# A diffusion block on one core: the input projection's first chunk in one written order with eight banks, its weights on GpSimd's queue, and another order of the first norm and dots

## The chip, the cores and the metric

The kernel runs on one core of a Trainium2 chip, in one launch. The metric is the device time of one execution in microseconds. The engines are TensorE (PE: matmuls; its weight loads are listed as PEld), VectorE (DVE), ScalarE (ACT), GpSimd (POOL) and SyncE (SP), which here only issues DMAs; GpSimd and ScalarE can issue them too.

## What is computed

One block of a latent transformer in f32 with 512 latent tokens, 256 context tokens and a width of 2048. What matters here is its start:

```python
mod_l = silu(c) @ w_ada + b_ada          # 6 * 2048 values: shift, scale, gate, twice
mod_c = silu(c_ctx) @ w_ada + b_ada
h_l = rms_norm(x, g_mix_norm) * (1 + sc_a) + sh_a       # 512 x 2048
p = h_l @ w_in                                          # 512 x 3904
```

Behind it come the context's part of the projection, attention, short convolutions, the output projection with a residual, and a gated MLP with a second norm; the change does not touch how they are written.

## The kernel before

**Matmuls.** Tokens are the free dimension (512), features lie on the 128 partitions, so x is 16 tiles of 128x512 (`xr0` to `xr15`). Each f32 operand is split into a high and a low part, and a product is three matmuls (`mm3`): high by high (L187), high by low of h (L188), low by high (L189). A weight tile that has landed is cut into pieces of up to 512 columns; ScalarE casts a piece to its high part (L166) and VectorE subtracts it from the raw tile for the low part (L167). The pieces have 4 buffers, and one more that every fifth uses.

**The first norm.** x lands in 16 loads on SP's queue; ScalarE squares each (L351, L354), VectorE adds them up (L355), TensorE sums over the partitions (L316), ScalarE takes the root (L289), VectorE the reciprocal (L291), TensorE spreads it over the partitions (L299), and ScalarE copies the result to `rl`.

**The shifts and scales.** Rows 16+j and j of `w_ada` (scale and shift of tile j) are not multiplied on TensorE: each comes as two halves of 128x1024 (`ada`, 4 buffers), and VectorE takes the dot with silu(c), which lies on all partitions as `sv`, in one instruction for each half (L241); `total` (L235) adds the halves and the bias. `prep(j)` does that for both rows and then makes h of tile j: VectorE multiplies by `rl` (L435), ScalarE applies scale and shift (L438) and casts to the high part (L337), VectorE makes the low part (L338). silu of c (and of c_ctx, as `svc`) is made by four matmuls that spread the row (L413) and four activations (L414).

**The input projection** has 31 blocks of 128 columns and 16 k-tiles. The k-tiles are taken in three chunks of 2, 4 and 10 (`KCH`). In each chunk the first G = 6 blocks go k-tile by k-tile into six banks (`pf`, from `first_banks`), as their h comes; the other 25 go block by block (`pp`). `evac` copies (chunk 0, ScalarE, L539) or adds (chunks 1 and 2, VectorE, L541) a full bank to `acc`. `prep` calls stand between the blocks of chunks 0 and 1; between those of chunk 2 stand the same dots with silu(c_ctx), for the context (L530).

**What sets the order.** A scheduler orders each engine's instructions; an instruction marked with `keep` stays in the written order among the others so marked on its engine. All loads of the first two chunks are kept on SP's queue, in the order of the calls:

```python
raw = load(w_in[:, off:off + k * P], k * P, f"rw{ci}_{m}")   # SP: fetch_to
...
for f, j in todo.get((ci, i), []):
    f(j)                          # prep: four ada loads on SP, then the dots
```

Of the kernel before, what the change touches and what calls it, by code (L numbers as in the profile page):

```python
# [10 lines left out]
F32 = mybir.dt.float32  # L11
# [20 lines left out]
G = 6  # L32

# [39 lines left out]
def block_kernel(ctx, tc, xt, ctxt, ctxn, c, c_ctx, w_ada, small, w_in, w_inc, w_q, w_kv, w_out,  # L73
# [38 lines left out]
    def big(nm):  # L112
        return pp.tile([P, 1024], F32, tag="b", bufs=2, name=nm)
# [15 lines left out]
    def first_banks(nm):  # L129
        turn[:] = 5, None  # L130
        r = [sml(f"{nm}{g}") for g in range(4)]
        b = big(f"{nm}4")
        return r + [b[:, :512], b[:, 512:]]
# [9 lines left out]
    def fetch_to(dst, src):  # L143

        ins = SP.dma_start(dst, src)
        if ordered[0]:
            keep(ins)

    def load(src, n, name):
        nth["raw"] += 1  # L150
        if "raw" in spare and nth["raw"] % 3 == 0:
            raw = spare["raw"].tile([P, 2048], F32, tag="raw", bufs=1, name=name)
        else:
            raw = wp.tile([P, 2048], F32, tag="raw", bufs=2, name=name)
        fetch_to(raw[:, :n], src)
        return raw
# [76 lines left out]
    def total(col, t, dst):  # L233

        V.scalar_tensor_tensor(out=dst, in0=col[:, 0:1], scalar=col[:, 1:2], in1=s("b_ada", t), op0=ALU.add, op1=ALU.add)  # L235

    def dot_v(raw, vec, t, dst, nm):

        col = tiny(2, f"dv{nm}{t}")
        for i, r in enumerate(raw):  # L240
            V.scalar_tensor_tensor(out=r, in0=r, scalar=1.0, in1=vec[:, i * 1024:(i + 1) * 1024], op0=ALU.mult, op1=ALU.mult, accum_out=col[:, i:i + 1])  # L241
        total(col, t, dst)
# [157 lines left out]
    with ExitStack() as pa:  # L400
# [4 lines left out]
        def silu_rows(src, dst, nm):  # L405

            row = wp.tile([P, 2048], F32, tag="raw", bufs=2, name=nm)[0:1, :]
            fetch_to(row, src)
            for g in range(4):
                if g % 2 == 0:  # L410
                    both = big(f"{nm}{g}")
                ps = both[:, (g % 2) * 512:(g % 2 + 1) * 512]
                PE.matmul(ps, ones[0:1, :], row[:, g * 512:(g + 1) * 512], start=True, stop=True)  # L413
                A.activation(dst[:, g * 512:(g + 1) * 512], ps, AF.Silu)  # L414
# [7 lines left out]
        hl = {}  # L422

# [28 lines left out]
        rms([ssq], D, T, rl)
        A.copy(out=ones_r, in_=ones)

        V.tensor_scalar(s("g_q", 0, 4), s("g_q", 0, 4), scalar1=-SCALE, scalar2=None, op0=ALU.mult)
# [101 lines left out]
        todo = {(0, 1 + 6 * i): [(prep, 2 + i)] for i in range(4)}  # L557
# [5 lines left out]
        off = 0  # L563
        for ci, (k0, n) in enumerate(zip(K0, KCH)):

            pss = first_banks(f"pf{ci}")
            if ci == 2:
                bg.append(ctx_stats())
            for q in range(n):
                if ci == 0:  # L570
                    prep(q)
                elif ci == 2:
# [436 lines left out]
    SP.dma_start(sv_d, sv)  # L1009
# [577 lines left out]
def _layout(x, c, ctx, c_ctx, w_ada, b_ada, g_mix_norm, w_in, g_q_a, w_q_b, g_kv_a, w_kv_b,  # L1587
# [25 lines left out]
    for t in range(8):  # L1613
# [57 lines left out]
```

## Time and profile before

| | |
|---|---|
| median of 3 runs | 2134.2 us (2133.86 to 2139.27) |
| the profiled execution | 2139.37 us, its span 2137.6 us |
| granted clock, mean of the span | 0.993 |
| TensorE busy | 2091.0 us of the span |
| VectorE busy | 1826.5 us |
| ScalarE busy | 1047.5 us |
| GpSimd busy | 117.2 us |

The span is the part of the profiled execution that the trace covers. The trace gives for each instruction its start, its duration, and what ended the idle time of its engine before it. "DMA share" is the mean busy share of the core's 16 DMA engines; PEclk is the clock that TensorE was granted, 1.00 being 2.4 GHz and 0.50 being 1.2 GHz.

### The profile page before, as it was taken

The page shows a single profiled execution, that of the slowest core. Times are in us where ns is not written, and L with a number is a line of the kernel's source. Part 1 is how long each engine was busy: PE and PEld are TensorE (multiplying, and loading weights), DVE is VectorE, ACT ScalarE, POOL GpSimd, SP SyncE. Part 2 cuts the span into 40 slices and gives each one's busy share as a digit, 9 for nine tenths or more (in the row PEclk, how much of TensorE's full clock was granted, in tenths as well). Part 3 has the DMA queues.
Part 4 walks back from the last instruction along what each step waited for, and adds up shares of the span by engine and source line. Part 5 has one row for each costly group of instructions (what it writes and reads, how often), then busy time and mean ns, then how long its engine had stood idle before and what let it go on. Part 6 is the DMA issues. An engine that isn't in the chain of part 4 may idle for free.

```text
span 2137.6 us, 35318 instructions
## 1 busy us (share of the span) xinstructions
PE 2091.0 (98%) x13268; PEld 1881.8 (88%) x13268; DVE 1826.5 (85%) x3024; ACT 1047.5 (49%) x1715; POOL 117.2 (5%) x144
## 2 busy tenths in 40 slices
PE   7999999999999999999999999999999999999997
PEld 4688788888988888999999999999999889999997
DVE  7998987778896989898999999999999658888887
ACT  5533333555552337565555555555655433333445
POOL 0000000000000100011000000000000000000000
PEclk9999999999999999999999999999999999999999
DMA  8989886334459986577788888788888989878684
GB/s 331 343 279 329 276 275 195 126 128 152 166 188 353 348 283 220 142 217 207 230 238 232 233 233 244 224 234 234 235 229 229 362 306 307 250 231 239 197 236 134
DMA packets 170177, 513.75 MB, mean 240 GB/s; under 512 B 18963, under 2 KB 23315, under 8 KB 164371
## 3 DMA queue, kind: packets, MB, share of 16 engines
q1 hardware_dynamic: 133364, 418.14, 57.7%
q0 software_dynamic: 17408, 59.25, 14.1%
q10 hardware_dynamic: 19232, 34.09, 4.2%
q8 instruction: 104, 1.70, 0.3%
q14 instruction: 69, 0.56, 0.1%
HBM read 464.22 MB, written 46.14 MB: 239 GB/s over the span
## 4 chain that ended last, share of the span: by engine, by line
PE 90%; DVE 4%; DMA 3%; ACT 2%; issue 1%; SPq 0%; DVEq 0%; ACTq 0%; POOLq 0%
PE pp L187 4%; PE pp L189 4%; PE pp L188 4%; PE d L187 1%; PE o L187 1%; PE d L188 1%; PE o L188 1%; PE d L189 1%; PE o L189 1%; PE uf L187 1%; PE uf L189 1%; PE uf L188 1%; PE of L187 1%; PE of L188 1%; PE of L189 1%; PE pf L188 1%
## 5 line engine op out<-in xcount | busy, mean ns | idle before, releaser
L1151 POOL DMA_DIRECT2D u_s<-in_w_up x80 | 68.6, 857 | 684.0 <-DMA u_s<-in_w_up 378.1
L263 DVE SCALAR_TENSOR_TENSOR ada<-ada,sv 128x1024 f32<-128x1024 f32 x68 | 82.1, 1220 | 11.4 <-DMA ada<-in_w_ada 11.2
L166 ACT CAST w_0h<-rw 128x512 fp32r<-128x512 f32 (+1 forms) x63 | 38.3, 618 | 108.3 <-PE pp L188 67.6
L241 DVE SCALAR_TENSOR_TENSOR ada<-ada,sv 128x1024 f32<-128x1024 f32 x64 | 77.6, 1220 | 2.2 <-DMA ada<-in_w_ada 2.1
L530 DVE SCALAR_TENSOR_TENSOR ada<-ada,svc 128x1024 f32<-128x1024 f32 x64 | 76.0, 1219 | 2.5 <-DMA ada<-in_w_ada 2.4
L167 DVE TENSOR_TENSOR w_0l<-rw,w_0h 128x512 fp32r<-128x512 f32 (+1 forms) x63 | 42.7, 683 | 22.8 <-ACT w_0h L166 22.6
L263 DVE SCALAR_TENSOR_TENSOR ra<-ra,sv 128x1024 f32<-128x1024 f32 x44 | 52.5, 1219 | 1.1 <-DMA ra<-in_w_ada 1.1
L1265 DVE TENSOR_TENSOR u<-u,u_s 128x1024 f32<-128x1024 f32 x40 | 48.8, 1220 | 0.7 <-DMA u_s<-in_w_up 0.5
L1266 DVE TENSOR_TENSOR u<-u,u 128x1024 f32<-128x1024 f32 x40 | 48.7, 1218 | 0.0
L793 POOL TENSOR_TENSOR gr<-gr,half 128x8 f32<-128x8 f32 x4 | 10.1, 2524 | 630.1 <-DVE gr L792 538.2
L764 ACT CAST pth<-t 128x384 fp32r<-128x384 f32 x64 | 28.6, 485 | 26.4 <-PE t L761 26.4
L1075 DVE TENSOR_TENSOR tp<-a,tp 128x256 fp32r<-128x256 f32 x90 | 37.7, 419 | 3.3 <-ACT tp L1074 3.3
L1074 ACT CAST tp<-a 128x256 fp32r<-128x256 f32 x90 | 35.7, 403 | 5.5 <-DMA yl6h<-y_d 4.2
L1038 ACT ACTIVATE g<-g 128x512 f32<-128x512 f32 x43 | 27.3, 634 | 18.3 <-DVE g L1032 18.0
L541 DVE TENSOR_TENSOR acc<-acc,pp 128x512 f32<-128x512 f32 x50 | 34.1, 683 | 2.1 <-PE pp L189 2.1
L765 DVE TENSOR_TENSOR ptl<-t,pth 128x384 fp32r<-128x384 f32 x64 | 33.2, 550 | 2.6 <-ACT pth L764 2.6
L745 DVE TENSOR_REDUCE mn<-s 128x1 f32<-128x768 f32 x32 | 30.4, 953 | 4.9 <-PE s L734 4.6
L1030 ACT ACTIVATE g<-cg,sm 128x512 f32<-128x512 f32 x40 | 32.6, 815 | 0.0
L1030 ACT ACTIVATE a<-ca,sm 128x512 f32<-128x512 f32 x40 | 32.1, 802 | 0.0
L748 ACT ACTIVATE p<-s,mn 128x768 f32<-128x768 f32 x32 | 29.3, 916 | 1.6 <-DVE mn L745 1.3
L1031 DVE SCALAR_TENSOR_TENSOR g<-cg,sm,g 128x511 f32<-128x511 f32 x40 | 29.8, 746 | 0.0
L1032 DVE SCALAR_TENSOR_TENSOR g<-cg,sm,g 128x511 f32<-128x511 f32 x40 | 29.8, 746 | 0.0
(10238 smaller groups left out, 8925.0 us busy)
## 6 DMA issues: line engine op xcount, KB each, us to landing
ada<-in_w_ada SPq DMA_DIRECT2D x196, 512.0 KB, 5.7
u<-in_w_up SPq DMA_DIRECT2D x120, 512.0 KB, 8.9
w<-t_d SPq DMA_DIRECT2D x161, 256.0 KB, 5.3
u_s<-in_w_up SPq DMA_DIRECT2D x80, 512.0 KB, 4.0
u_s<-in_w_up POOLq DMA_DIRECT2D x80, 512.0 KB, 9.6
t_d<-tp ACTq DMA_DIRECT2D x126, 256.0 KB, 5.9
v<-in_w_dnw SPq DMA_DIRECT2D x72, 384.0 KB, 5.1
ra<-in_w_ada SPq DMA_DIRECT2D x22, 1024.0 KB, 4.8
```

The lines of the kernel that those rows point to most:

```text
L166: A.copy(out=hi[:, :n], in_=raw[:, a:a + n])
L167: V.tensor_tensor(out=lo[:, :n], in0=raw[:, a:a + n], in1=hi[:, :n].bitcast(F32), op=ALU.subtract)
L187: PE.matmul(ps, w[0], x[0], start=first, stop=False, skip_group_check=on_top)
L188: PE.matmul(ps, w[0], x[1], start=False, stop=False, skip_group_check=on_top)
L189: PE.matmul(ps, w[1], x[0], start=False, stop=last, skip_group_check=on_top)
L241: V.scalar_tensor_tensor(out=r, in0=r, scalar=1.0, in1=vec[:, i * 1024:(i + 1) * 1024], op0=ALU.mult, op1=ALU.mult, accum_out=col[:, i:i + 1])
L263: keep(V.scalar_tensor_tensor(out=r, in0=r, scalar=1.0, in1=svs[i], op0=ALU.mult, op1=ALU.mult, accum_out=lc[:, t % 4:t % 4 + 1] if i else ...
L530: keep(V.scalar_tensor_tensor(out=raw[q], in0=raw[q], scalar=1.0, in1=svc[:, q * 1024:(q + 1) * 1024], op0=ALU.mult, op1=ALU.mult, accum_o ...
L1030: A.activation(u, src, AF.Identity, bias=s("fb", m), scale=s("fw", 86 + m))
L1151: G_.dma_start(r[-1], src[more], accum_op=ALU.add)
L1265: V.tensor_tensor(out=a11, in0=a11, in1=s1, op=ALU.add)
L1266: V.tensor_tensor(out=a12, in0=a12, in1=a11, op=ALU.add)
```

## The change

- **Chunk 0** is written as one stream of 128x512 pieces (`groups`, `split_group`), all kept: 8 blocks go k-tile by k-tile into eight banks (`GCH`), then 23 blocks one by one. The weights in DRAM are laid out to match. The first load of weights stays on SP's queue (in two halves); the three others are issued on GpSimd's queue, the first of them behind a copy on GpSimd (`late`) that waits for `mod[:, 17]`.
- **First norm.** The x loads go first on SP's queue; `io` and `c` go on ScalarE's. The sum of squares is kept in two parts, tiles 0 to 13 and 14 to 15, each with its own sums on TensorE. VectorE multiplies tile 0 by the spread reciprocal straight from its bank. ScalarE makes the high parts of h0 and h1 in one activation ahead of the full-precision result. Two tiny activations call up the tables of Silu and Sqrt early. The small constants come in two loads.
- **First dots.** Their halves are loaded up to four ahead, one by one, and the dots stand in the written order among the adds.
- **TensorE** gets 29 matmuls of a copy of x's first tile by ones, into a bank that nobody reads (`warm_up`), between the sums and the transposes.
- **c_ctx** is loaded on all partitions at once (1 MB, a broadcast read) and put through one Silu of 128x2048 in chunk 1, in place of four matmuls and four activations at the start. The store of `sv` for later use is kept behind its place in the written order.

```diff
+GCH = [8, 6, 6]
-    def load(src, n, name):
+    def load(src, n, name, E=None, halves=False):
...
-        fetch_to(raw[:, :n], src)
+        if E is not None:
+            keep(E.dma_start(raw[:, :n], src))
...
+        def scaled(j):
...
+                keep(V.tensor_tensor(out=x, in0=x, in1=rl, op=ALU.mult))
+            hl[j] = tuple(t2([P, T], F32R, f"h{j}{z}") for z in "hl")
+            if j < 2:
+                keep(A.activation(hl[j][0], x, AF.Identity, bias=mod[:, j:j + 1], scale=sc))
+            keep(A.activation(x, x, AF.Identity, bias=mod[:, j:j + 1], scale=sc))
...
+        while len(xs) < 12:
+            x_load_in()
+        ada_half()
+        while len(xs) < NK:
+            x_load_in()
+        fetch_to(sm[:, :112], small[:, :112])
+        for _ in range(3):
+            ada_half()
+        raw0 = load(w_in[:, :2 * GCH[0] * P], 2 * GCH[0] * P, "rf00", halves=True)
...
+        def warm_up(n):
+            for _ in range(n):
+                keep(PE.matmul(idle[:, :512], ones_r, warm, start=True, stop=True))
...
+            if j == 13:
+                dot(16, 0)
+                warm_up(4)
+                sums(parts[0], True, False)
+                warm_up(3)
+            elif 8 <= j:
+                warm_up(2)
+        keep(A.activation(tiny(1, "root"), eps, AF.Sqrt))
+        sums(parts[1], False, True)
...
+        dot(16, 1)
+        dot(0, 0)
+        warm_up(1)
+        keep(V.reciprocal(rr, rr))
...
+        warm_up(7)
+        dot(0, 1, lambda: keep(V.tensor_tensor(out=xs[0], in0=xs[0], in1=rs[:, 512:], op=ALU.mult)))
...
+        def split_group(i):
+            ci, bs, off, size, b = stream[i]
+            if off not in raws:
+                raws[off] = load(w_in[:, off:off + size * P], size * P, f"rw{off}", G_)
...
+        for i, (ci, bs, off, size, b) in enumerate(stream):
+            if i < 2:
+                for _ in range(2):
+                    next(one)
+                if i == 1:
+                    keep(G_.tensor_copy(out=tiny(1, "late"), in_=mod[:, 17:18]))
+            else:
+                for n in range(len(ready), min({2: 4}.get(i, i + 3), len(stream))):
+                    split_group(n)
...
+        def context_row(i):
+            if i == 0:
+                fetch_to(svc, c_ctx[0].partition_broadcast(P))
+                keep(V.tensor_scalar(s("g_q", 0, 4), s("g_q", 0, 4), scalar1=-SCALE, scalar2=None, op0=ALU.mult))
+            else:
+                keep(A.activation(svc, svc, AF.Silu))
...
+        todo[1, 13] = [(context_row, 0)]
+        todo[1, 19] = [(context_row, 1)]
```

**Where it moves instructions.** On SP's queue, from the first dots' loads on, the order before is this (`rf` is the first load of weights, `rw_13` and `rw_21` the next two, `ada` the halves of rows of `w_ada`):

```order
L145 DMA rf_251<-in_w_in 128x1536
L1009 DMA sv_d<-sv 128x2048
L145 DMA ada_283<-in_w_ada 128x1024
L145 DMA ada_285<-in_w_ada 128x1024
L145 DMA ada_291<-in_w_ada 128x1024
L145 DMA ada_293<-in_w_ada 128x1024
L145 DMA rw_13_337<-in_w_in 128x2048
L145 DMA ada_360<-in_w_ada 128x1024
...
L145 DMA ada_459<-in_w_ada 128x1024
L145 DMA rw_21_473<-in_w_in 128x2048
```

Now the same stretch of SP's queue holds this, up to the first `ada` half for tile 2:

```order
L148 DMA rf_155<-in_w_in 128x1024
L148 DMA svc<-in_c_ctx 128x2048
L148 DMA ada_268<-in_w_ada 128x1024
L148 DMA ada_270<-in_w_ada 128x1024
L148 DMA ada_272<-in_w_ada 128x1024
L148 DMA ada_274<-in_w_ada 128x1024
L148 DMA rf_155<-in_w_in 128x1024
L148 DMA sm<-in_small 128x430
L148 DMA ada_362<-in_w_ada 128x1024
```

And GpSimd's own instructions begin with the copy and the three loads:

```order
L725 COPY late<-mod 128x1
L159 DMA rw_370<-in_w_in 128x2048
L159 DMA rw_471<-in_w_in 128x2048
L159 DMA rw_587<-in_w_in 128x1792
```

The `rw` loads have left SP's queue, whose `ada` loads now follow each other; the scheduler has put the load of `svc` ahead of four of them.

On VectorE, from the first low part of h on, the order before is this (`h0l` and `h1l` are the low parts of tiles 0 and 1, `w_13_0l` a low part of weights):

```order
L338 TENSOR_TENSOR h0l<-xr_113,h0h 128x512
L241 SCALAR_TENSOR_TENSOR ada_285,dvl_287<-ada_285,sv 128x1024
L241 SCALAR_TENSOR_TENSOR ada_291,dvl_295<-ada_291,sv 128x1024
...
L241 SCALAR_TENSOR_TENSOR ada_293,dvl_295<-ada_293,sv 128x1024
L235 SCALAR_TENSOR_TENSOR mod<-dvl_295,sm 128x1
L435 TENSOR_TENSOR xr_117<-xr_117,rl 128x512
L167 TENSOR_TENSOR w_13_0l<-rw_13_337,w_13_0h 128x512
L167 TENSOR_TENSOR w_15_0l<-rw_13_337,w_15_0h 128x512
L241 SCALAR_TENSOR_TENSOR ada_360,dvl_364<-ada_360,sv 128x1024
L167 TENSOR_TENSOR w_17_0l<-rw_13_337,w_17_0h 128x512
L338 TENSOR_TENSOR h1l<-xr_117,h1h 128x512
```

Now VectorE has in that place (`w2l` and `w3l` are of the first load, `w4l` and `w5l` of the first of GpSimd's):

```order
L493 TENSOR_TENSOR h0l<-xr_114,h0h 128x512
L702 TENSOR_TENSOR w1l<-rf_155,w1h 128x512
...
L482 TENSOR_TENSOR xr_116<-xr_116,rl 128x512
L702 TENSOR_TENSOR w2l<-rf_155,w2h 128x512
L493 TENSOR_TENSOR h1l<-xr_116,h1h 128x512
L702 TENSOR_TENSOR w3l<-rf_155,w3h 128x512
L471 SCALAR_TENSOR_TENSOR ada_362,dv_364<-ada_362,sv 128x1024
L471 SCALAR_TENSOR_TENSOR ada_366,dv_364<-ada_366,sv 128x1024
L243 SCALAR_TENSOR_TENSOR mod<-dv_364,sm 128x1
L702 TENSOR_TENSOR w4l<-rw_370,w4h 128x512
L702 TENSOR_TENSOR w5l<-rw_370,w5h 128x512
```

The low parts of later weights have moved behind tile 1's h and two more dots, in a fixed place.

## Rows read from the trace of the kernel before

**Rows 1.** The page's first part: busy time and share of the span, by engine.

```profile
PE 2091.0 (98%) x13268; PEld 1881.8 (88%) x13268; DVE 1826.5 (85%) x3024; ACT 1047.5 (49%) x1715; POOL 117.2 (5%) x144
```

**Rows 2.** Windows: stretch and length (us), engines' busy time, PEclk, DMA share, GB/s.

```profile
core 0: us, PE busy (x) PEld busy (x) DVE busy (x) ACT busy (x) POOL busy (x), PEclk, DMA share, GB/s
0.00:29.63 29.63, 17.60 (x29) 7.18 (x29) 19.49 (x37) 21.02 (x35) 0.20 (x4) 1.00 0.94 353
29.63:81.33 51.70, 45.48 (x165) 33.85 (x166) 44.64 (x90) 25.01 (x47) 0.00 (x0) 0.93 0.86 310
81.33:168.74 87.41, 86.45 (x373) 69.78 (x372) 86.02 (x162) 32.77 (x55) 0.00 (x0) 1.00 0.86 307
168.74:205.90 37.16, 37.16 (x162) 30.13 (x161) 29.98 (x61) 16.94 (x30) 0.00 (x0) 1.00 0.93 330
205.90:252.40 46.50, 45.44 (x201) 36.73 (x200) 43.22 (x84) 13.97 (x25) 0.00 (x0) 1.00 0.85 296
252.40:312.81 60.41, 60.41 (x278) 49.59 (x276) 52.66 (x105) 21.03 (x40) 0.00 (x0) 1.00 0.81 273
640.00:2137.00 1497.00, 1479.18 (x10160) 1374.88 (x10158) 1284.19 (x2005) 753.85 (x1147) 107.60 (x137) 1.00 0.81 244
```

**Rows 3.** Waits of TensorE, 90 to 320 us: total, times, longest (us).

```profile
PE pp L189 <- DVE w_0l L167: 1.6, 2, 1.1
```

**Rows 4.** Timeline at 313 us: start, duration, engine, operation, idle before.

```profile
312.81 0.68 DVE L167 TENSOR_TENSOR w_0l<-rw,w_0h 128x512 fp32r<-128x512 f32 x1
...
313.55 0.51 PE L189 MATMUL pp<-h6h,w_0l 128*128 128x512 f32 x1 [0.56 <-DVE w_0l L167]
```

**Rows 5.** Timeline of TensorE: the first of chunk 0, and the change to chunk 1.

```profile
29.63 2.07 PE L187 MATMUL pf<-h0h,wf_0h 128*128 128x512 f32 x4 [3.21 <-ACT h0h L337]
...
86.18 0.39 PE L187 MATMUL pf<-h2h,wf_0h 128*128 128x512 f32 x1
86.41 0.39 PE L188 MATMUL pf<-h2l,wf_0h 128*128 128x512 f32 x1
...
90.36 0.40 PE L187 MATMUL pf<-h4h,wf_0h 128*128 128x512 f32 x1
```

**Rows 6.** Chain that ended last, 0 to 33 us: start, duration, what.

```profile
17.43 0.70 DVE xs0t L355
...
30.30 2.29 DVE ada L241 x4
```

**Rows 7.** Waits of SP's queue, 0 to 81.33 us: total, times, longest.

```profile
SPq L145 <- DVE ada L241: 36.8, 18, 4.7
```

**Rows 8.** Timeline of SP's queue from 25 us.

```profile
29.25 14.62 SPq L145 DMA_DIRECT2D ada<-in_w_ada  x8
43.96 0.38 SPq L145 DMA_DIRECT2D rw<-in_w_in  x1
```

**Rows 9.** Waits of VectorE, 81.33 to 312.81 us.

```profile
DVE w_0l L167 <- ACT w_0h L166: 7.7, 6, 3.1
```

**Rows 10.** Timeline of ScalarE at 180 us.

```profile
178.92 0.62 ACT L166 CAST wf_8h<-rf 128x512 fp32r<-128x512 f32 x1 [1.17 <-PE pf L188]
180.72 0.62 ACT L166 CAST wf_0h<-rf 128x512 fp32r<-128x512 f32 x1 [1.18 <-PE pf L188]
...
185.14 0.62 ACT L166 CAST wf_8h<-rf 128x512 fp32r<-128x512 f32 x1 [0.82 <-PE pf L188]
```

**Rows 11.** Groups of ScalarE by form: count, busy, mean ns.

```profile
L438 ACT ACTIVATE xr<-xr,mod,sc 128x512 f32<-128x512 f32 x16 | 12.9, 814 | 9.9 <-DVE xr L435 9.9
...
L414 ACT ACTIVATE svc<-cc 128x512 f32<-128x512 f32 x4 | 2.4, 597 | 3.9 <-PE cc L413 3.9
...
L414 ACT ACT_TABLE_LOAD x1 | 1.3, 1283 | 0.0
```

**Rows 12.** DMA issues: count, KB each, median us from issue to landing.

```profile
u_s<-in_w_up SPq DMA_DIRECT2D x80, 512.0 KB, 4.0
u_s<-in_w_up POOLq DMA_DIRECT2D x80, 512.0 KB, 9.6
```

More of the change, by code (lines that the diff above doesn't have):

```diff
@@ L127, in bank, with first_banks @@
         return b[:, :512]
[L129 to L130 removed]
+    def first_banks(nm, n):
+        turn[:] = (5 if n == 6 else 0), None
         r = [sml(f"{nm}{g}") for g in range(4)]
[L132 to L133 removed]
+        for g in range(4, n, 2):
+            b = big(f"{nm}{g}")
+            r += [b[:, :512], b[:, 512:]]
+        return r
     def bc(ap, n):
@@ L403, in block_kernel, with broadcast_row @@
         spare["w"] = p_sb, 1, 5
-        def silu_rows(src, dst, nm):
+        def broadcast_row(src, nm):
             row = wp.tile([P, 2048], F32, tag="raw", bufs=2, name=nm)[0:1, :]
-            fetch_to(row, src)
+            A.dma_start(row, src)
+            r = [sml(f"{nm}{g}") for g in range(4)]
             for g in range(4):
[L410 to L414, printed above, removed]
+                PE.matmul(r[g], ones[0:1, :], row[:, g * 512:(g + 1) * 512], start=True, stop=True)
+            return r
         def ada_load(t):
@@ new lines, in block_kernel, with low, preps @@
+        done = set()
+        def low(j):
+            keep(V.tensor_tensor(out=hl[j][1], in0=xs[j], in1=hl[j][0].bitcast(F32), op=ALU.subtract))
+            done.add(j)
+        def preps(js):
+            for j in js:
+                for t in (16 + j, j):
+                    for i in range(2):
+                        dot(t, i)
+                        if (t, i) == (j, 1):
+                            scaled(j)
+                        yield
+                low(j)
+                yield
+        A.dma_start(io, consts[:, KCW:])
@@ new lines, in block_kernel, with sums @@
+        rs = big("rs")
+        idle = big("idle")
+        def warm_up(n):
+            for _ in range(n):
+                keep(PE.matmul(idle[:, :512], ones_r, warm, start=True, stop=True))
+        def sums(q, first, last):
+            for g in range(4):
+                keep(PE.matmul(rs[:, g:g + 1], q[:, g * P:(g + 1) * P], ones[:, 0:1], start=first and g == 0, stop=last and g == 3))
+        parts = []
+        for j in range(NK):
+            q = tmp([P, T], F32, f"xs{j}")
+            keep(A.activation(q, xs[j], AF.Square))
+            if j in (0, 14):
+                parts.append(q)
+            else:
+                keep(V.tensor_tensor(out=parts[-1], in0=parts[-1], in1=q, op=ALU.add))
+            if j in (2, 4, 6, 8):
+                g = j // 2 - 1
+                keep(A.activation(sv[:, g * 512:(g + 1) * 512], cps[g], AF.Silu))
+            if j == 13:
[5 more added lines that the diff above has]
+                warm_up(2)
@@ L457, in block_kernel @@
+        sc0 = tiny(1, "sc0")
+        keep(V.scalar_tensor_tensor(out=sc0, in0=mod[:, 16:17], scalar=1.0, in1=s("g_mix", 0), op0=ALU.add, op1=ALU.mult))
+        for _ in range(4):
+            ada_half()
+        n = GCH[0] * P
+        fetch_to(raw0[:, n:2 * n], w_in[:, n:2 * n])
+        fetch_to(sm[:, 112:], small[:, 112:])
         qan, kvl, krl, kvc, krc = [], [], [], [], []
@@ L554, in evac, with groups @@
                 late_bg.append(gn_apply((m - 9) // 3, acc[m]))
-        todo = {(0, 1 + 6 * i): [(prep, 2 + i)] for i in range(4)}
+        def groups():
+            off = 0
+            for ci, (k0, n) in enumerate(zip(K0[:1], KCH)):
+                g = GCH[ci]
+                rows = [(q, m) for q in range(n) for m in ORDER[:g]]
+                rest = [(q, m) for m in ORDER[g:] for q in range(n)]
+                for bs, per in ((rows, 2 * g), (rest, 16)):
+                    for a in range(0, len(bs), per):
+                        size = min(per, len(bs) - a)
+                        for b in range(0, size, 4):
+                            yield ci, bs[a + b:a + min(b + 4, size)], off, size, b
+                        off += size * P
+            offs.append(off)
```

136 lines of the change are left out of this document (112 added, 24 removed).

## The prediction

> **What bounds the kernel now.** I read the page's totals first. TensorE is busy 98% of the span, VectorE 85% [rows 1]. So TensorE is idle for some 47 us, and the second view, the windows by stage [rows 2], says where: 18.3 us up to 81.33 us (12.03 + 6.22), and 17.8 spread over the 1497 us behind 640. What is gained ahead of 640 us is carried to the end there, since TensorE is full; nothing is added. From 29.63 to 312.81 us it is also nearly full, but so is VectorE: 86.02 of 87.41 us in one stretch, 43.22 of 46.50 in another. Two engines are at their limit, and the question is which of them ends last.
>
> The waits of TensorE answer that. Between 90 and 320 us it waits twice in all, both times for a low part of weights from VectorE [rows 3]. The second is at 313.55 us, behind the subtraction that VectorE starts at 312.81 [rows 4]. Ahead of that place TensorE is paced by VectorE, behind it by itself. So I take the place at 312.81 us as the one that decides: the change gains what makes this subtraction start earlier, up to what TensorE can gain itself.
>
> How early can VectorE be there? I counted its instructions ahead of this subtraction in the order of both kernels, and priced them by this trace's rows (two dots with what belongs to them take 2.29 us, 1.145 each [rows 6]; a 128x512 subtraction 0.68 [rows 4]). That gives 277.1 us before and 277.2 after: one add of squares is gone, a cast of 128x512 has come. The work is the same, so only VectorE's idle time can shrink. By the windows it is idle for 81.33 − 19.49 − 44.64 = 17.2 us up to 81.33 us, then 1.4, 7.2, 3.3 and 7.75 us in the four stretches up to 312.81, together 36.8 us [rows 2].
>
> **TensorE's own gain, the cap.** Before, the first matmul of chunk 0 starts at 29.63 us, after waiting for h0's high part [rows 5]. In the new order, VectorE's last add of squares, which before starts at 17.43 us and ends at 18.13 [rows 6], ends at about 18.3: half an `ada` row comes ahead of the last four tiles on SP's queue, but `io` has left it. Behind it stand three dots (3 × 1.145), then the small instructions and the product of tile 0 (about 1.1 with the 0.68 of a subtraction), then ScalarE's activation (0.81 [rows 11]), and about 1 us of handing over: 24.6 us, 5 earlier. The end of chunk 0 before is 90.36 us, but 12 matmuls of chunk 1 had been done by then (the stretch from 86.18 us on); at the pitch of 0.23 us [rows 5] that makes 87.6 like for like. After, walking through the written order (about 10 us of VectorE for each k-tile of h, TensorE's matmuls between) I get 72.6 to 75 us, a lead of 12 to 15 us. About 3 us of it go at once, because TensorE then waits for the first low parts of chunk 1, so I take 12.0 as the cap.
>
> TensorE's clock: the first matmuls of chunk 0 took 2.07 us for four, against a pitch of 0.23 later [rows 5], and the granted clock of that stretch is 0.93 on the mean, under 1.00 elsewhere [rows 2]. The warm-up matmuls run in time in which TensorE has nothing to do. The excess that they could save is 2.07 − 4 × 0.23 = 1.15 us for these four, and at most 0.07 × 51.7 = 3.6 us for the stretch; VectorE doesn't move by it, I cost them at nothing. Their cover is VectorE's dots, which end later; without it the 29 would cost 29 × 0.23 = 6.7 us of TensorE.
>
> **VectorE's idle time, stretch by stretch.**
>
> *Up to 81.33 us.* Of the two kernels' orders, the one after reaches the first piece of chunk 1 with 5 dots and 7.6 us less work done ahead of it than before (54.0 against 61.6 us), because dots have moved behind. In my walk VectorE starts there at 71.6 us. With the 7.6 us that were put off this is 79.2 us against 81.33: 2.1 us gained. It is so little against TensorE's 12 because VectorE hardly idled there for anything but the norm: 17.2 us, against 15.1 after. From below: in the walk VectorE waits a little for weights at each stop of the order, and if the weights are late or the order is stiffer than I think, 5 us are lost. From above: if none of these waits comes, 6 are gained.
>
> This is where the loads on GpSimd's queue count. SP's queue stands for VectorE's dots for 36.8 us up to 81.33 [rows 7]: the load at 43.96 is behind eight `ada` loads, which take 14.62 us to issue since each waits for a buffer that a dot must free [rows 8]. The three loads skip that. The first is held back by `late` until row 17's total, about 30 us in my walk, and its low part comes up on VectorE at 39.3 us: it has 8.5 us to land. The second is issued at about 37.8 and due at 49.2, the third at 47.9, due at 61.2: 11.4 and 13.3 us. A load of 512 KB takes 4.0 us from issue to landing on SP's queue and 9.6 on GpSimd's later in this kernel, where many are on the way [rows 12]. These are 1 MB and 0.9 MB; the core moved 353 GB/s in the first stretch [rows 2], so 1 MB is 3 us alone. I take 8 us, which costs nothing, from between 3 and twice 9.6 = 19.2, and nearest to the single 9.6, since little else is in flight at that time.
>
> The Trainium skill, page "DMA: Bandwidth & Descriptors", section "Issuing engines are not separate DMA queues", says that all DMAs run on the same 16 engines whoever issues them, and that issuing from several engines saves only the time of the issue itself. By that rule the three loads would be worth three issues of 0.38 us, 1.1 us together, and the rest of the gain would have to come from the order. The trace disagrees in this respect: what stands on SP's queue is its wait for dots, 36.8 us, not the issue.
>
> *81.33 to 168.74 us.* The new Silu of 128x2048 and a table load stand on ScalarE ahead of a tile's activation and a cast of weights. By rows: a table load 1.28 us, and 2.4 us for the same 2048 columns in four pieces [rows 11]. Some 3.5 us stand in ScalarE's queue, and VectorE's low part behind that cast is late by what ScalarE isn't ahead. ScalarE is idle over half of this stretch (32.77 of 87.41 busy [rows 2]), so I take 1.0 us lost, from between none and 3.5. In return the start loses four matmuls and four activations; they lay under the wait for x, worth nothing.
>
> *168.74 to 205.90 us.* VectorE idles 7.2 us there. Three casts of weights waited for TensorE to free their buffer, 1.17 + 1.18 + 0.82 = 3.2 us [rows 10], and VectorE's low parts wait for such casts (7.7 us in 6 waits over the four stretches [rows 9]). With TensorE ahead by its lead, these casts are free in time. I take 3.2, from between 0 (VectorE then waits for the next thing, the load) and 5.
>
> *205.90 to 312.81 us.* 3.3 + 7.75 = 11.0 us idle. From the same reason, I take the part for which TensorE is the cause as 3.4 us, from between 0 and 5.5; the rest waits for `rw` and `ada` loads, which are the same as before.
>
> **The sum:** 2.1 − 1.0 + 3.2 + 3.4 = 7.7 us, below the cap of 12.0. Behind 312.81 us the orders are practically the same. The profiled execution took 2139.37 us and would take 2131.7; that one was the slowest of the three shown, and the median is 2134.2, so I forecast 2134.2 − 7.7 = **2126.5 us**. A difference under 0.3%, 6.4 us here, is about what a measurement of this kernel can't tell from none.
>
> **The rivals.**
>
> *TensorE keeps its whole lead.* If VectorE's waits of 36.8 us shrink by 12 or more, since all of those on TensorE and on late casts go with the lead, the cap is what counts: 2134.2 − 12 = 2122 us. For it: VectorE waits for ScalarE's casts, not for loads, in most of its waits [rows 9]. Against it: little idle time is left ahead of 81.33 us to take.
>
> *Little comes through.* The stretch to 81.33 gives nothing or costs a little, the Silu costs 3, and VectorE's idle time of 168 to 313 us is a wait for loads that takes the place of the wait for TensorE: 0 to 4 us gained, 2132 us. For it: VectorE had only 17.2 us of idle time at the start, most of which the loading of x makes; the DMA share is 0.81 to 0.93 in all four stretches [rows 2], so loads can well be next.
>
> *GpSimd's loads land late (slower).* The low parts are in a fixed order on VectorE now, so a late load holds up all dots behind it, and by that SP's `ada` loads too. Landing after L us costs (L − 8.5) + (L − 11.4) + (L − 13.3) against the due times above. From L = 13.6 this is the whole gain of 7.7; from 15.7 the kernel is slower by more than 6.4. At 17 it costs 17.8 − 7.7 = 10.1: 2144 us. For it: 9.6 us for half the size on this queue, more than twice SP's 4.0 [rows 12]. Against it: that was with loads from both queues in flight, and three loads only. The Trainium skill, page "SBUF — State Buffer", speaks for it: GpSimd's queue has its descriptors written by GpSimd, which certain copies of VectorE lock out. No row here shows that; GpSimd issued its 80 loads of the later stage while VectorE was busy [rows 2].
>
> **How the numbers follow.** The forecast has a chance of 0.40, its own range 2123 to 2131, and about three quarters of it are beyond 6.4 us; the whole lead 0.22; little 0.22; late loads 0.16. Faster: 0.30 + 0.22 = 0.52. Same: 0.10 + 0.22 = 0.32. Slower: 0.16. The range leaves out the worse half of late loads and the end of the whole lead where chunk 1's wait doesn't come either (15 us and more): 2118 to 2139.
>
> **What the profile would show.** Right: the first real matmul at about 24.6 us, tile 1's at 35, the end of chunk 0 at 73 to 76, VectorE's idle time up to chunk 1 near 15 us, new waits of TensorE for low parts at the start of chunk 1 and in chunk 2, and the casts of wf at 180 us without a wait for TensorE. Wrong: waits of ScalarE's casts for the `rw` loads of chunk 0, landings over 13 us on GpSimd's queue, a granted clock of 0.50 through a good part of chunk 0, or a place behind 313 us where the trace of the change loses or gains against this one.

## The result: slower, by little

The changed kernel takes 2139.8 us, the median of 18 runs (2134.2 to 2142.8); the kernel before takes 2134.5 (2133.1 to 2139.3) on the same chip. The ratio is 1.002, with an interval of 1.0013 to 1.0027: 2.8 to 5.8 us slower, which is still inside the 0.3% (6.4 us) that the prediction took as no change, against 7.7 us faster in the forecast. The profiled execution of before, 2139.37 us, lies 4.9 us above the median of its kernel, that of the change, 2140.52, only 0.75 above. So the two traces are compared stage by stage, and no total is taken from them.

The start went almost as the prediction's walk had it. TensorE's timeline of the changed kernel (start, duration, operation, idle before and who ended it; against [rows 5]):

```profile
24.28 1.19 PE L747 MATMUL pf<-h0h,w0h 128*128 128x512 f32 x4 [0.48 <-ACT h0h L485]
...
34.80 1.83 PE L747 MATMUL pf<-h1h,w2h 128*128 128x512 f32 x4 [4.68 <-ACT w2h L701]
...
81.47 0.50 PE L195 MATMUL pf<-h4h,wf_0h 128*128 128x512 f32 x1 [3.13 <-ACT wf_0h L174]
...
221.30 0.51 PE L197 MATMUL pp<-h6h,w_0l 128*128 128x512 f32 x1 [2.51 <-DVE w_0l L175]
```

The first matmul is at 24.28 us (24.6 was expected), tile 1's at 34.80 (35), the last of chunk 0 at 76.07 (73 to 76). Chunk 0 has 186 matmuls, and the 186th matmul of the projection starts at 75.14 us against 87.34 before: like for like a lead of 12.2 us, the lower end of the 12 to 15 of the walk. Then the lead goes, at 81.47 us first. The cast that TensorE waits for there had itself waited for a load of chunk 1's weights, and behind the wait the granted clock is 0.80. ScalarE's cast, and the window behind the wait (columns as in [rows 2]):

```profile
80.80 0.62 ACT L174 CAST wf_0h<-rf 128x512 fp32r<-128x512 f32 x1 [5.46 <-DMA rf<-in_w_in]
```

```profile
81.47:90.00 8.53, 8.40 (x29) 6.10 (x30) 7.38 (x15) 6.25 (x11) 0.00 (x0) 0.80 1.01 391
```

At 221.30 us TensorE waits again, now for a low part from VectorE. GpSimd's loads were in time. GpSimd's timeline, and ScalarE's cast behind the first of them:

```profile
30.45 0.70 POOL L159 DMA_DIRECT2D rw<-in_w_in  x1
36.99 0.55 POOL L159 DMA_DIRECT2D rw<-in_w_in  x1 [5.84 <-DVE w3l L702]
48.50 0.53 POOL L159 DMA_DIRECT2D rw<-in_w_in  x1 [10.96 <-DVE w7l L702]
...
38.98 0.62 ACT L701 CAST w4h<-rw 128x512 fp32r<-128x512 f32 x1 [3.71 <-DMA rw<-in_w_in]
```

The load issued at 30.45 lets its cast start at 38.98, 8.5 us later (8 was taken), and the low part follows at 39.63 (39.3 in the walk). VectorE is where the forecast fails. Its timeline in the changed kernel, the first low part of chunk 1 and that of chunk 2's third block:

```profile
74.32 0.69 DVE L175 TENSOR_TENSOR wf_0l<-rf,wf_0h 128x512 fp32r<-128x512 f32 x1 [0.76 <-ACT wf_0h L174]
...
220.56 0.69 DVE L175 TENSOR_TENSOR w_0l<-rw,w_0h 128x512 fp32r<-128x512 f32 x1
```

The same two in the kernel before are at 81.33 and 223.97 us. The windows of both between these places (stretch, engines' busy time, PEclk, DMA share), those of before cut anew from 168.74 on, the others being in [rows 2]:

```profile
168.74:223.97 55.23, 54.91 (x238) 44.20 (x236) 46.78 (x90) 21.83 (x39) 0.00 (x0) 1.00 0.92 331
223.97:312.81 88.84, 88.10 (x400) 72.26 (x400) 79.07 (x157) 30.11 (x56) 0.00 (x0) 1.00 0.81 273
```

And of the changed kernel:

```profile
0.00:74.32 74.32, 63.13 (x239) 46.04 (x239) 56.43 (x108) 44.38 (x81) 3.03 (x8) 0.98 0.89 328
74.32:169.84 95.52, 91.29 (x380) 71.94 (x381) 92.81 (x179) 36.77 (x57) 0.00 (x0) 0.98 0.85 301
169.84:220.56 50.72, 48.95 (x211) 39.04 (x209) 41.86 (x82) 22.08 (x37) 0.00 (x0) 1.00 0.91 318
220.56:310.80 90.24, 89.45 (x394) 72.51 (x394) 84.38 (x169) 29.42 (x56) 0.00 (x0) 0.98 0.85 294
...
221.30:230.00 8.70, 8.70 (x31) 6.94 (x32) 8.70 (x15) 2.26 (x4) 0.00 (x0) 0.80 0.74 252
```

VectorE idles 17.9, 2.7, 8.9 and 5.9 us in these four stretches, 35.3 in all; before it was 17.2, 1.4, 8.4 and 9.8, 36.8. It saved 1.5 us of idle time, not 7.7, and starts the subtraction that before stands at 312.81 us at 310.71, 2.1 us earlier. (The last window ends at 310.80, which is 312.81 less TensorE's lead behind that place.)

How far TensorE is ahead of the profiled execution of before can be read by taking the start of the same matmul in both timelines. Negative is ahead, in us, by the time in the trace of before:

| execution | 97 | 200 | 320 | 643 | 805 | 835 | 1590 | 2120 |
|---|---|---|---|---|---|---|---|---|
| changed | −6.4 | −5.0 | −2.0 | −3.1 | −2.9 | +0.3 | +0.3 | +0.8 |
| e1 | −6.5 | −5.4 | +2.6 | +0.1 | +0.8 | +3.1 | +3.1 | +3.1 |
| e2 (before, store late) | −3.3 | −3.3 | −3.3 | −4.4 | −4.4 | −2.0 | −2.0 | −3.2 |
| e4 (before again) | −1.2 | −0.8 | −1.2 | −0.9 | −0.9 | −0.3 | −0.3 | −1.3 |
| e8 (before, no context dots) | 0.0 | +0.4 | −1.6 | −4.0 | −3.4 | −0.4 | −0.4 | −3.5 |
| e9 (changed, no context dots) | −7.9 | −6.5 | −8.5 | −11.6 | −11.4 | −9.1 | −9.1 | −9.2 |
| e10 | −6.2 | −5.1 | −0.8 | −3.6 | −3.3 | +0.1 | +0.1 | +2.4 |
| e13 | −8.7 | −7.4 | −5.3 | +4.4 | +4.4 | +7.1 | +7.1 | +10.1 |
| e15 | −9.0 | −8.0 | −4.5 | −7.4 | −7.4 | −3.3 | −3.3 | −4.0 |
| e17 | −7.8 | −6.3 | −3.3 | −6.0 | −6.0 | −4.9 | −4.8 | −9.0 |

In chunk 2, between 200 and 320 us, the changed kernel loses 3.0 us of its lead, and e1, whose order on the four compute engines is the same up to there, 8. Up to 205 us e10, e12 and e13 have this order too, and the leads of the five at 200 us lie between 5.0 and 7.4 us: a difference of 2.4 us there is scatter between single executions. At the start of the MLP, between 805 and 835 us, it loses what is left.

### The profile page after: what moved, and what is told of

The parts are those of the page before. It is cut to its first block, busy times and chain, and to the rows that moved or that the text cites. A ratio compares the mean times of both kernels' runs of the same rounds, so it can differ in the third digit from the quotient of the medians.

```text
span 2138.7 us, 35361 instructions
## 1 busy us (share of the span) xinstructions
PE 2090.1 (98%) x13297; PEld 1881.5 (88%) x13297; DVE 1823.6 (85%) x3024; ACT 1049.5 (49%) x1715; POOL 119.6 (6%) x148
## 4 chain that ended last, share of the span: by engine, by line
PE 85%; DVE 6%; DMA 5%; ACT 2%; issue 1%; SPq 0%; DVEq 0%; ACTq 0%; POOLq 0%
PE pp L195 3%; PE pp L196 3%; PE pp L197 3%; PE d L195 1%; PE o L197 1%; PE d L196 1%; PE o L195 1%; PE d L197 1%; PE o L196 1%; PE uf L195 1%; PE uf L196 1%; PE of L195 1%; PE uf L197 1%; PE of L197 1%; PE of L196 1%
## 5 line engine op out<-in xcount | busy, mean ns | idle before, releaser
L273 DVE SCALAR_TENSOR_TENSOR ada<-ada,sv 128x1024 f32<-128x1024 f32 x68 | 82.2, 1220 | 6.5 <-DMA ada<-in_w_ada 6.4
L174 ACT CAST w_0h<-rw 128x512 fp32r<-128x512 f32 x50 | 30.9, 620 | 92.5 <-PE pp L196 53.0
L249 DVE SCALAR_TENSOR_TENSOR ada<-ada,sv 128x1024 f32<-128x1024 f32 x40 | 48.8, 1222 | 1.0 <-DMA ada<-in_w_ada 1.0
L175 DVE TENSOR_TENSOR w_0l<-rw,w_0h 128x512 fp32r<-128x512 f32 x50 | 34.4, 688 | 11.3 <-ACT w_0h L174 10.3
L1005 POOL TENSOR_TENSOR gr<-gr,half 128x8 f32<-128x8 f32 x4 | 10.1, 2525 | 579.0 <-DVE gr L1004 487.2
```

Source lines behind the costliest of these rows:

```text
L249: ins = V.scalar_tensor_tensor(out=r, in0=r, scalar=1.0, in1=vec[:, i * 1024:(i + 1) * 1024], op0=ALU.mult, op1=ALU.mult, accum_out=col[:, ...
L273: keep(V.scalar_tensor_tensor(out=r, in0=r, scalar=1.0, in1=svs[i], op0=ALU.mult, op1=ALU.mult, accum_out=lc[:, t % 4:t % 4 + 1] if i else ...
```

## The experiments

Four theories were put against each other. Theory 1: the moved store of `sv` gives the lead back. Theory 2: the output projection's dots end at the same time whatever came before. Theory 3: the new order of chunk 2's loads on SP's queue gives the lead back. Theory 4: VectorE's work in chunk 2, above all the context's dots, does. Ratios are to the kernel before on the same chip, with 95% intervals.

**e1, e2: the moved store.** The store of `sv` now stands between the last dots' loads and the MLP's first weights on SP's queue, so it was the first suspect.

```diff
-    keep(SP.dma_start(sv_d, sv))          # behind the output projection
+        keep(SP.dma_start(sv_d, sv))      # e1: behind the input projection
```

e1, the changed kernel with the store put there: 

> The changed kernel with the store of sv issued behind the input projection instead of behind the last dots of the output projection. In the changed kernel TensorE is 3.1 us ahead of before at 643 us and 0.2 behind at 816: the first weights of the MLP stand behind that store on SP's queue. Theory 1 (the store is what gives the lead back): the lead of about 3 us passes 816 us, and the kernel comes out 3 to 6 us below the changed one, 2134 to 2137. Theory 2 (the output projection's dots and their loads end at the same time whatever came before, the store is harmless): no change, 2138 to 2141.

 e2, the kernel before with the store where the change has it: 

> The kernel before with only the store of sv moved to where the changed kernel has it. Theory 1: 3 to 6 us slower than before, the first weights of the MLP issued 2 to 3 us later. Theory 2: no change.

e1 took 2137.6 us, 1.0013 (1.0002 to 1.0025); e2 2134.5, 0.9994 (0.9982 to 1.0007). Moving the store alone costs nothing that can be measured. e1 lies 2.1 us below the changed kernel, between what the two theories wanted, and the intervals of the two overlap. In the table e2 is 3.3 us ahead from the start, where its store of 1 MB is not issued, and gives 2.4 of it back at 805 to 835. e1 loses 2.3 us at that place too, without the store. So the store is not what gives the lead back, and theory 1 falls.

**e3: the Silu of 128x2048 in chunk 1.** The call that issues it is left out. 

> As e1, and without the Silu of 128x2048 in chunk 1, so the context's shifts and scales are made from c_ctx itself. If that Silu and its table load are what costs VectorE its lead in chunk 1, VectorE is about 3 us earlier at the end of chunk 1 than in e1, and the kernel up to 3 us faster than e1; if not, it equals e1 within 1 us.

 It took 2137.9 us, 1.0014 (1.0001 to 1.0028): as e1, and TensorE's lead at 170 us is 4.3 us, no more than e1's 5.4. My 1.0 us for it was not found.

**e4: the kernel before once more.** 

> The kernel before once more, for a second profiled execution: its first one lies 4.9 us above the median of 18. Whatever lies between the two executions of one kernel is not the change. I expect up to 5 us of difference behind 640 us and less than 0.5 ahead of it.

 It took 2138.0 us in one execution. Against the first it is 1.2 us ahead from the start on and 1.3 at the end; against my expectation, the difference came ahead of 640 us.

**e5: the load of c_ctx later.**

```diff
-                fetch_to(svc, c_ctx[0].partition_broadcast(P))
+                    if n == len(stream) - 4:      # behind the three loads of weights
+                        keep(G_.dma_start(svc, c_ctx[0].partition_broadcast(P)))
```

> As e1, and the 1 MB load of c_ctx goes on GpSimd's queue behind the three loads of weights instead of on SP's queue at 15.5 us. In the changed kernel the second half of the first weights and four halves of w_ada stand behind it, and VectorE waits 2.2 us for the cast of that half. If VectorE's order sets the pace from there, VectorE reaches chunk 1 about 2.5 us earlier than in e1 and TensorE is 2 to 3 us earlier at the end of chunk 1 (5.4 us ahead of before in e1, so 7.5 to 8). If the loads of chunk 0 set it, no change at chunk 1. Total 2135 to 2138.

 It took 2138.2 us, 1.0018 (1.0007 to 1.0029). TensorE was 6.5 us ahead at 170 us, 1.1 more than e1 and half of what I expected, and 0.9 at 320: gained in the start, lost in chunk 2.

**e6, e7: the loads of chunk 2 in the written order; low parts a dot later.** e6 sets `ordered[0] = False` only behind chunk 2. e7 also calls `low(j)` one `yield` later. 

> As e5, and the loads of chunks 1 and 2 stay in the written order on SP's queue. In e1 and the changed kernel 8 halves of w_ada stand between two loads of weights in chunk 2, 4 before, and TensorE waits 2.5 us at 253 us in e1 for a cast behind that load. Theory 3 (the new order of chunk 2's loads gives the lead back): TensorE keeps at 320 us the lead that it has at 200, 5 us or more, and the kernel is 3 to 5 us faster than e5. Theory 4 (VectorE's own work sets the place): the same waits come at other places, the lead at 320 us is that of e5 within 1 us.

 

> As e6, and the low part of h of tiles 2 to 4 stands one dot later on VectorE. In the changed kernel VectorE waits 1.5 us for ScalarE at each of three of them. Theory 4 (VectorE sets the pace): VectorE is 4 to 4.5 us earlier at chunk 1 and this stays to 320 us, so the kernel is 3 to 4.5 us faster than e6. If TensorE or the loads set the pace, no change.

Both are far off, 2259.2 us (1.0588, 1.0573 to 1.0603) and 2267.8 (1.0625, 1.0611 to 1.0639). TensorE's waits in e6, 75 to 330 us (total, times, longest):

```profile
PE pp L195 <- ACT w_0h L174: 38.3, 8, 12.2
PE pf L195 <- ACT wf_0h L174: 19.9, 5, 8.7
```

In that order each load of weights stands behind the halves of `w_ada` of the block ahead, whose buffers wait for dots: between 170 and 330 us SP's queue waits 118.8 us in all for them. It tells nothing on theory 3 but that the scheduler's order of these loads is worth some 120 us. e7 showed one more thing, in VectorE's waits of its chunk 0:

```profile
DVE w9l L707 <- ACT w9h L706: 2.1, 1, 2.1
DVE w11l L707 <- ACT w11h L706: 2.0, 1, 2.0
```

The 1.5 us at the low parts of h had become 2 us at the low parts of weights, whose casts stand on ScalarE behind the same activation. The waits had moved, not gone.

**e8, e9: both kernels without the context's dots.**

```diff
-keep(V.scalar_tensor_tensor(out=raw[q], in0=raw[q], scalar=1.0, in1=svc[...], op0=ALU.mult, op1=ALU.mult, accum_out=d))
+keep(V.tensor_tensor(out=d, in0=raw[q][:, :1], in1=svc[:, q:q + 1], op=ALU.mult))
```

> The kernel before with the 128 dots of the context (w_ada by silu of c_ctx, between the blocks of chunk 2 and behind) replaced by a product of one column each, which still reads the load and frees its buffer; the context's shifts and scales are left out by that. VectorE has some 60 us less to do ahead of 312 us. To be read against e9.

 

> e1 with the same dots replaced. Theory 4 (VectorE's work in chunk 2 takes the lead): without it TensorE keeps to 320 us the 5 us by which it leads at 200 us, so e9 is 4 to 6 us ahead of e8 there. If loads take it, e9 gives the lead back at the same places, and is within 2 us of e8 at 320 us.

 (There are 64 such dots; "128" in the first is my slip.)

e8 took 2135.4 us, 1.0006 (0.9996 to 1.0017); e9 2130.5, 0.9977 (0.9962 to 0.9992). The windows of e8, then of e9:

```profile
206.00:252.00 46.00, 46.00 (x204) 37.38 (x204) 26.14 (x65) 14.21 (x25) 0.00 (x0) 1.00 0.86 301
252.00:313.00 61.00, 61.00 (x280) 50.13 (x280) 34.95 (x94) 21.60 (x41) 0.00 (x0) 1.00 0.76 269
```

```profile
206.00:252.00 46.00, 46.00 (x209) 37.61 (x208) 29.37 (x73) 15.05 (x26) 0.00 (x0) 1.00 0.94 332
252.00:313.00 61.00, 61.00 (x277) 49.97 (x276) 31.79 (x86) 20.89 (x40) 0.00 (x0) 1.00 0.83 293
```

With the dots gone TensorE is full in both. e9's lead over e8 is 6.9 us at 200 us, 6.9 at 320 and 5.7 at the end (the table), 4.9 by the medians, and the two intervals don't meet. With the dots in place the changed start is worth nothing. This is the pair that decides: the dots in chunk 2 take the lead (theory 4). The pair takes out VectorE's work together with the time for which the dots hold their loads' buffers; which of the two counts is for the next runs. The kernel before hardly waits for the dots: without them its trace gains 2.0 us between 200 and 320 us, and its median is no faster.

**e10, e11, e12: VectorE relieved, or the loads moved.** e10 (changed) and e11 (before) make the 128x256 low parts of chunk 2 on GpSimd; e12 issues the weights' loads of chunk 2's blocks on GpSimd's queue.

```diff
-        V.tensor_tensor(out=lo[:, :n], in0=raw[:, a:a + n], ...)
+        (G_ if n in low_on else V).tensor_tensor(out=lo[:, :n], in0=raw[:, a:a + n], ...)   # low_on = [256] in chunk 2
-                    raw = load(w_in[:, off:off + k * P], k * P, f"rw{ci}_{m}")
+                    raw = load(w_in[:, off:off + k * P], k * P, f"rw{ci}_{m}", G_ if ci == 2 else None)   # e12 alone
```

> e1, and the low parts of the last two k-tiles of each block of chunk 2 (128x256, 25 pieces of 0.42 us, 10 us of VectorE) are made on GpSimd. Theory 4 (VectorE's work in chunk 2 takes TensorE's lead): the lead of 5 us at 200 us is kept to 320 us within 2 us, and the kernel is 3 to 6 us faster than e1 (2137.6), below before. Rival (weights' loads that stand behind halves of w_ada on SP's queue take it): TensorE's waits for casts at 250 us stay, and the time is that of e1. If GpSimd takes more than about 5 us for a piece, it becomes what TensorE waits for and both lose.

 

> The kernel before with the same pieces on GpSimd. TensorE has no lead to lose there and waits 1.6 us in all for VectorE in chunk 2 before: at most 1.6 us faster, or no change.

 

> e1, and the weights of chunk 2's blocks are loaded on GpSimd's queue, so they don't stand behind halves of w_ada on SP's. Rival of theory 4 (the loads' place on SP's queue): the waits for casts at 250 us go, the lead of 5 us is kept, 3 to 5 us faster than e1. Theory 4: TensorE's waits for low parts from VectorE take their place, the lead at 320 us is at most VectorE's 3.4 us, and the time is within 2 us of e1.

e10 took 2136.1 us, 1.0006 (0.9995 to 1.0017), e11 2135.8, 0.9997 (0.9985 to 1.0009), e12 2137.9, 1.0015 (1.0003 to 1.0028). e12's waits of TensorE are still those for VectorE and for casts:

```profile
220.06 0.50 PE L197 MATMUL pp<-h6h,w_0l 128*128 128x512 f32 x1 [2.88 <-DVE w_0l L175]
...
252.36 0.50 PE L195 MATMUL pp<-h6h,w_0h 128*128 128x512 f32 x1 [1.25 <-ACT w_0h L174]
```

So the place of the weights' loads on SP's queue is not what takes the lead; theory 3 falls. The Trainium skill, page "DMA: Bandwidth & Descriptors", section "Issuing engines are not separate DMA queues", holds that another issuing engine saves only the time of the issue; e12 agrees here, with 0.2 us between it and e1, while e6 shows what an order within one queue can cost. e10 is 1.5 us below e1, within the scatter, where 3 to 6 were expected: only 15 of the 25 pieces lie ahead of 320 us, 6.3 us of VectorE's work, VectorE was still busy 44.69 of 46 us from 206 to 252, and TensorE went from 5.1 us ahead to 0.8. That it is VectorE's time, and not the buffers, that the dots take is therefore argued, from e12 and from the wait for a low part at 221.30 us; the run that should have shown it did not.

**e13, e14: the dots thinner.** One step behind each block of chunk 2 instead of one or two.

```diff
-                    for q in range(2 if i % 4 == 0 else 1):
-                        next(cm, None)
+                    next(cm, None)
```

> e1, and chunk 2 takes one step of the context's dots behind each block instead of one or two (7 steps, 14 dots of 1.14 us, move behind the last blocks, where VectorE is idle 20 of 87 us). Theory 4 (VectorE's work between 206 and 313 us takes the lead): VectorE has 4 to 6 us less to do up to 252 us, TensorE's wait at 220 us shrinks from 2.3 to below 1, the lead at 320 us is 3 us or more, and the kernel is 2 to 4 us faster than e1. If the waits come from something else, no change.

 

> The kernel before with the same edit: TensorE waits 1.6 us there in all, so at most 1.6 us faster, or no change.

Slower: 2147.6 us, 1.0058 (1.0042 to 1.0075), and 2142.7, 1.0040 (1.0026 to 1.0054). e13 is 5.3 us ahead at 320, as theory 4 says, but this does not show it. Its order departs from e1's only at 233 us. Its lead was 7.4 us at 200 us already, and its wait at 218.59 us is 2.28 us, not below 1. The dots put off are then due in the next stage. A line of e13's waits of TensorE, 100 to 430 us:

```profile
PE qr L389 <- ACT xq L864: 5.4, 1, 5.4
```

(In the changed kernel this wait is 1.0 us.) By 643 us it is 4.4 behind; that the dots put off are the cause is read from this and from e14, not tested apart. The density of the dots in chunk 2 has a bound on its other side.

**e15 to e18: no warm-up, and two versions.** e15 makes `warm_up` return at once. e16 is e13 with e10, e5 and the later low parts. e17 is e15 with e10; e18 is e17 with e5.

> e1 without the 29 warm-up matmuls. By the prediction they are worth nothing: the first matmuls of chunk 0 run at the lower clock again (2 us for four), the lead at the end of chunk 0 shrinks by 1 to 3 us, and nothing of that is left at 200 us or in the time, since VectorE sets the pace. If they count, 2 us slower than e1.

 

> e13 with the small low parts on GpSimd (e10), the load of c_ctx on GpSimd's queue (e5) and the low parts of tiles 2 to 4 a dot later (as in e7, without its order of loads). By theory 4 each frees VectorE: 10 us in chunk 2 and up to 4 us in the start; the lead at 320 us is 5 us or more, and the kernel is 4 to 6 us faster than e1, 2 to 4 below before. If the later stages take any lead, no faster than before.

 

> e15 (no warm-up matmuls, the store of sv behind the projection) with the small low parts of chunk 2 on GpSimd as in e10, which was 1.5 us faster than e1. Theory 4: a lead of 4 to 6 us at 320 us, and 2132 to 2135, at or up to 3 us below before. If e15's gain was chance, 2136 as e10.

 

> e17 with the load of c_ctx on GpSimd's queue behind the weights (e5, which was 1.1 us further ahead at 170 us than e1). If that counts, 1 us faster than e17; else the same.

e15 took 2135.5 us, 1.0003 (0.9991 to 1.0014). Its TensorE timeline beside that of the change above:

```profile
24.21 2.07 PE L746 MATMUL pf<-h0h,w0h 128*128 128x512 f32 x4 [1.83 <-ACT h0h L485]
...
34.74 2.06 PE L746 MATMUL pf<-h1h,w2h 128*128 128x512 f32 x4 [2.98 <-ACT w2h L700]
```

Without the warm-up the first four matmuls take 2.07 us instead of 1.19, as before the change [rows 5], and the wait for the next weights shrinks from 4.68 to 2.98. Tile 1 starts at 34.74 against 34.80: the warm-up only lengthens a wait. e16 took 2150.9 us, 1.0075 (1.0060 to 1.0091): in chunk 0 TensorE waited 4.1, 3.1 and 2.5 us for pieces of weights behind the later low parts, and it is 4.0 us behind before at 200 us where e13 is 7.4 ahead; the thinner dots cost it 8 more up to 450 us, as they cost e13. e17 took **2131.9 us, 0.9987 (0.9978 to 0.9995)**, below both kernels, and e18 2132.7, 0.9987 (0.9974 to 0.9999): c_ctx's load does not count.

## Why the prediction was wrong

**Right.** The place of the first matmul, of tile 1, of the end of chunk 0 with its lead of 12.2 us, the landing of GpSimd's load, the warm-up at nothing, and that TensorE's lead counts only as far as VectorE follows.

**Wrong: the sum of VectorE's idle time.** Of 7.7 us, 1.5 came.
- *Up to 81.33 us*, 2.1 gained: measured 0.7 lost (17.9 against 17.2 us idle). The walk had VectorE at chunk 1 at 71.6 us; it was there at 74.32. The changed kernel's waits of VectorE, 0 to 74.32 us:

```profile
DVE w2l L702 <- ACT w2h L701: 2.2, 1, 2.2
DVE h2l L493 <- ACT h2h L488: 1.5, 1, 1.5
DVE h3l L493 <- ACT h3h L488: 1.5, 1, 1.5
DVE h4l L493 <- ACT h4h L488: 1.5, 1, 1.5
```

  The written order puts each low part of h right behind the product that ScalarE must first work on, so VectorE stands 1.5 us at each of three. In the scheduler's order before there is one such wait among these tiles, of 2.6 us for the high part of tile 3.
- *81 to 169 us*, 1.0 lost: measured 1.3, but not for the Silu (e3).
- *169 to 313 us*, 6.6 gained: measured 3.5 in the two stretches together, all behind 220 us. The casts that I held to be freed by TensorE's lead still left VectorE waiting, 2.6 us for two of wf_4 and 2.3 for one of wf_8 between 169.84 and 220.56 us. And the casts still wait for TensorE to free their buffers, as long as before [rows 10]; TensorE's lead did not take that wait away:

```profile
178.25 0.62 ACT L174 CAST wf_4h<-rf 128x512 fp32r<-128x512 f32 x1 [1.24 <-PE pf L196]
180.11 0.62 ACT L174 CAST wf_8h<-rf 128x512 fp32r<-128x512 f32 x1 [1.25 <-PE pf L196]
```

**Wrong: the cap.** I took 12.0 us as TensorE's own gain, 15 less some 3 us for low parts at the start of chunk 1. The lead was 12.2, the wait there 3.13 us and for a load; with the lower clock behind it, 1.7 us (0.20 of 8.53), 6.4 us are left at 97 us and 5.0 at 200. So even with VectorE's 7.7 us TensorE had less than that to give.

**Wrong: what it costs when the lead runs into VectorE.** I had TensorE's lead cut down to VectorE's and no more. At 221.30 us TensorE waits 2.51 us, which takes its lead to VectorE's 3.4 us (223.97 − 220.56). Behind it the granted clock is 0.80 over 8.70 us, 1.7 us more, and 2.0 us are left at 320. The two waits of the kernel before in this stage, 1.06 and 0.56 us [rows 3, rows 4], cost no clock: it is 1.00 behind them. In e1 the same wait, of 2.29 us, costs no clock either, but a second, of 2.48 us at 252.85, is followed by 0.76 over 7.15 us and a third, of 1.03 us at 314.61, by 0.77 over 7.39, and it is 2.6 us behind before at 320. So a lead that can't be kept can be paid for twice.

**Half wrong: "what is gained ahead of 640 us is carried to the end".** At the start of the MLP TensorE waits for the second norm and for the first weights. It was 2.9 us ahead at 805 us and started the MLP at 815.98 us, against 815.83 before: all of it gone. 1.0 us went on the way to the MLP's first high part of h (`hf0h`), which is made 1.9 us earlier than before; the other 2.0 went behind it. ScalarE in the changed kernel, then before (`ufw0h` is the high part of the MLP's first weights):

```profile
812.78 0.39 ACT L1173 CAST hf0h<-x 128x256 fp32r<-128x256 f32 x1
...
814.83 0.37 ACT L337 COPY rl<-rs 128x256 f32<-128x256 f32 x1 [0.23 <-PE rs L309]
815.09 0.83 ACT L1235 CAST ufw0h<-ufr 128x768 fp32r<-128x768 f32 x1
```

```profile
814.66 0.39 ACT L961 CAST hf0h<-x 128x256 fp32r<-128x256 f32 x1
814.96 0.83 ACT L1023 CAST ufw0h<-ufr 128x768 fp32r<-128x768 f32 x1
```

In the changed kernel the scheduler has put four instructions between the two casts, before none; the first load of these weights is issued at 811.05 us, against 808.34. So the orders behind 312.81 us, which I had called practically the same, differ here. I had seen TensorE idle for 17.8 us behind 640 and called it spread; 3.7 of it are the two waits here. But this is no stop that swallows every lead, so theory 2 falls too: e9 and e17 pass it with 9.1 and 4.9 us in hand, and e13, which comes 4.4 us late, loses 2.7 as well. Against the first trace of before, all others lose 0.3 (e18) to 4.1 us (e15) at this place. Those that lose least, e18, e4 and e17, have the order of before between the two casts; e10, e11, e13 and e16 have it too and lose 2.5 to 3.4 us, with the last dots starting 1.6 to 3.0 us behind the last matmul of the output projection, 0.27 in before. No run moves one of the two alone.

**The rival that came nearest** is "little comes through". Its mechanism, a wait for loads in place of the wait for TensorE, is there at 81.47 us and not in the casts at 180 us, and it did not foresee a loss.

**What stays open.** The traces account for a change that is the same within 0.3%; the medians say 5.3 us slower. Between 1590 and 2120 us, where both kernels have the same code, the changed kernel, e1, e5, e10, e12, e13, e14 and e16 lose 0 to 3.0 us against the first trace of before; the others gain 0.1 to 4.2. Taking the warm-up away alone was worth 2.1 us by the medians (e15 against e1), and with e10's edit 4.2 (e17 against e10), of which the start shows 1 to 3 in the table. But the intervals of e15 and e1 overlap, those of e17 and e10 touch, and equal orders differ by 2.4 us at 200 us, so what of it is warm-up and what is chance was not settled.

## What to carry to other kernels

An engine's lead is worth what the engine that feeds it can follow in the next dense stage; look for that stage and leave its work out of both kernels, as e8 and e9 do, before working on the start. Idle time "caused by" a late engine is not saved by making that engine earlier: count it only where the next thing it would wait for is known to be there. And an order written by hand needs something between an instruction and what another engine must do before its result can be used.

## What the runs showed of the hardware

- Behind some waits of TensorE the granted clock was 0.76 to 0.80 for the next 7 to 9 us, that is a part of them at 1.2 GHz; behind others it was 1.00. The length of the wait doesn't tell them apart here: the first kind are waits of 3.13 and 2.51 us in the change, 2.28 in e13 (at 218.59 us), 2.48 and 1.03 in e1; the second kind are 2.29 in e1, 1.90 in e10 and 1.06 before. The windows behind e1's three (columns as in [rows 2]):

```profile
220.61:229.31 8.70, 8.70 (x37) 7.08 (x38) 8.70 (x15) 2.25 (x4) 0.00 (x0) 1.00 0.81 268
252.85:260.00 7.15, 7.15 (x24) 5.44 (x25) 7.15 (x12) 1.41 (x3) 0.00 (x0) 0.76 0.92 330
314.61:322.00 7.39, 7.39 (x25) 5.90 (x26) 6.20 (x13) 1.22 (x3) 0.00 (x0) 0.77 0.72 239
```

- Two executions of one order of instructions differ by 4.6 us at 320 us (the change and e1), more than most effects looked for; the verdicts above rest on the timed runs, and the table only shows where.
- GpSimd took 1.06 us for a 128x256 subtraction; VectorE takes 0.42. In e10's groups of GpSimd, 170 to 320 us (count, busy, mean ns, idle before):

```profile
L177 POOL TENSOR_TENSOR w_8l<-rw,w_8h 128x256 fp32r<-128x256 f32 x15 | 15.9, 1061 | 251.5 <-ACT w_8h L176 245.3 <-DVE ada L648 6.2
```

- TensorE's pace in the MLP's second half varies within an execution at a granted clock of 1.00: from 1900 to 2000 us the trace has 836 matmuls before and 846 in the change, but over all of 1590 to 2120 us the two stay within 0.5 us. What makes this 1% is not known.
